# Two expert positions of a mixture-of-experts block in column tiles of 32

## The chip, the cores and the metric

The kernel runs on one core of one Trainium2 chip. The metric is the device time of one execution in microseconds, the median of several runs. The profile is one further execution, taken by the hardware profiler.

## What is computed

The reference is one decoder layer on 512 tokens of width 1024: RMSNorm, an input projection, a pooling mixer and latent attention side by side, an output projection with residual, and then a mixture of experts with residual and a final RMSNorm. The part that matters here is the mixture:

```python
logits = (ht @ w_router + b_router).astype(jnp.float32)      # 32 experts
top_vals, top_idx = lax.top_k(logits, TOP_K)                  # 4 per token
gates = jax.nn.softmax(top_vals, axis=-1)
...
gu = xblk @ w_gate_up[e] + b_gate_up[e]                       # 1024 -> 2 x 1024
gate = jnp.minimum(gu[:, :D_EXPERT], SWIGLU_LIMIT)
up = jnp.clip(gu[:, D_EXPERT:], -SWIGLU_LIMIT, SWIGLU_LIMIT)
act = gate * jax.nn.sigmoid(SWIGLU_ALPHA * gate) * (up + 1)
return act @ w_down[e] + b_down[e]                            # 1024 -> 1024
```

Each expert works on the tokens that chose it, and its rows are added to those tokens, times the gate. All of it is float32. With the reference's inputs, the two experts that the last two positions get have 31 and 22 tokens.

## The kernel before

The mixer and attention take the first fifth of the time. After the routing, the experts are ranked by their number of tokens and put on 32 **positions**. `KINDS` gives each position a kind: the big ones ("B") have 104 or 128 slots for tokens, the small ones ("S") 64. Positions 0 and 1 are fixed experts, the twelve big positions come next by size and alternate with small ones, and positions 26 to 31 are all small, with position 31 (`E - 1`) the last. If an expert has more tokens than its position has slots, a loop at the end (`tc.For_i`) takes the rest in further blocks of 128; `capc` is the number of slots by rank.

A position has eight **gate-up items** (128 rows of `w_gate_up`, 1 MB each) and four **down items** (256 rows of `w_down`, 1 MB; for position 31, `load_down_last`, a half of the output columns and 512 rows each). The SP queue loads each item into one of nine slots, in a fixed order, as soon as a slot is free. A planner (`interleave`) writes the order of all items out by hand; TensorE (PE) keeps that program order (`InOrder`). Between items `step()` advances other work by one piece: the selection and the gathering of tokens, the transposes (`turn`), and the scatter pairs (`combine`: two matmuls add one pair of positions to 128 tokens by 512 columns, then DVE adds the result to `y`, line 1157).

In a small position a matmul has the tokens as its stationary operand, 64 columns wide, and a row block of the weights as the moving one, 512 columns at a time. Its output has 64 partitions, so two matmuls lie side by side in one PSUM bank: in `gate_up` the column blocks c = 0, 1 (gate) share one bank and c = 2, 3 (up) another, on partitions `64 * (c % 2)`. `swiglu` takes the two banks as 128 partitions by 512; `turn` transposes the result and copies it to `at` (line 1044), and `down` multiplies it with `w_down`, the two column halves q side by side in a bank `db`.

When a small position's four down items are done, ACT scales the two halves of `db` into `ysh` (line 1107), DVE takes the rest into `ysl` (line 1109) and writes the scatter matrices `ss0`, `ss1` (line 1105). Two small positions share these tiles: one has columns 0 to 511 on partitions 0 to 63, the other on 64 to 127. Position 30 (`E - 2`) has no partner, since position 31 is treated alone in `down_last`; DVE therefore writes zeros to the other half of the tiles first (line 1103). These tiles have one buffer, so the writes wait until the pair before (28 and 29) has been scattered.

`down_last` runs for position 31 and column half c = 0, then 1: eight matmuls into a bank, even k on partitions 0 to 63 and odd k on 64 to 127 as partial sums (the scatter adds them), eight scatter matmuls of position 30, the copies to `ybh` and `ybl`, eight scatter matmuls of position 31, the additions to `y` (line 1139) and the final norm (`final_norm`), ending with four writes of the output.

At the end, PE's order is: the last six of the 16 gate-up items of positions 30 and 31, each with a scatter pair of positions 28 and 29 behind it; the spreading of `g_final` (`spread`, four matmuls with one row); the seventh scatter pair; the transposes of position 30; its first down item; the eighth scatter pair; two down items; the transposes of position 31; the last down item; `down_last`.

Of the kernel before, what the change touches and what calls it, by code (L numbers as in the profile page):

```python
# [24 lines left out]
P = 128  # L25
# [102 lines left out]
def block_kernel(ctx: ExitStack, tc: tile.TileContext, xT, x, pos, vecs, w_in, w_pool, w_qb, w_kvb, w_out,  # L128
# [656 lines left out]
    def bank(tag):  # L785
        return pools["pm"].tile([P, T], F32, tag=tag, bufs={"x": 4, "y": 2, "m": 2}[tag], name=tag)
# [59 lines left out]
    def big(r):  # L846
        return r == "o" or KINDS[r] == "B"

    def slots_of(r):
        return CAP if r != "o" and big(r) and KINDS[:r].count("B") >= NFULL else P  # L850

    def onx(r):

        return big(r) or r == 0 or r == E - 1

    def select(r, ovc=None):

        oh = mo.tile([P, NT, P], F16, tag="oh", bufs=2, name="oh")
        src = ovc[:, :, 0] if r == "o" else posm[:, :, r]
        for t in range(NT):  # L860
            if big(r):
                n = slots_of(r)
                V.tensor_scalar(oh[:, t, 0:n], iota_s[:, 0:n], src[:, t:t + 1], None, op0=ALU.is_equal)
            else:
                V.tensor_scalar(oh[:, t, :].rearrange("p (a b) -> p a b", a=2),  # L865
                                iota_s[:, 0:64].unsqueeze(1).to_broadcast([P, 2, 64]), src[:, t:t + 1], None,
                                op0=ALU.is_equal)
        onehot[r] = oh

# [92 lines left out]
    def biases(r, cs):  # L962
        for c in cs:
            bs = bias[:, c * T:(c + 1) * T]
            if big(r):
                PE.matmul(banks[r][c], lhsT=m4b[0:96, r:r + 1].to_broadcast([96, slots_of(r)]), rhs=bs, start=True, stop=False)
            else:
                q = 64 * (c % 2)
                PE.matmul(banks[r][c // 2][q:q + 64, :], lhsT=m4b[0:96, r:r + 1].to_broadcast([96, 64]), rhs=bs,
                          start=not fixed(r), stop=fixed(r))  # L970

    def gate_up(r, k):

        first = r == "o"
        if k == 0:
            banks[r] = [bank("x" if onx(r) else "y")[0:slots_of(r)] for _ in range(4 if big(r) else 2)]
        if big(r):

            todo = [(hf, c) for hf in range(2) for c in range(2)] if k < KD - 1 else [
                (hf, c) for c in range(2) for hf in range(2)]  # L980
            parts = presplit.pop((r, "gu", k))
            for n, (hf, c) in enumerate(todo):
                cs = slice(c * T, (c + 1) * T)
                if k == 0 and not first:
                    biases(r, [2 * hf + c])
                mm3(PE, banks[r][2 * hf + c], xg[r][0][:, k, :], xg[r][1][:, k, :], parts[hf][0][:, cs],
                    parts[hf][1][:, cs], first and k == 0, k == KD - 1)
                if n == 1:
                    yield
        else:  # L990
            w = wslots.pop((r, "gu", k))
            for c in range(4):
                q = 64 * (c % 2)
                if k == 0 and c % 2 == 0 and not fixed(r):
                    biases(r, [c, c + 1])
                PE.matmul(banks[r][c // 2][q:q + 64, :], lhsT=xg[r][:, k, :], rhs=w[:, c * T:(c + 1) * T],
                          start=(k == 0 and fixed(r)), stop=(k == KD - 1 and not fixed(r)))

                if k == KD - 1 and c % 2 == 1 and fixed(r):
                    biases(r, [c - 1, c])  # L1000

    def swiglu(gb, ub, gbias=None, ubias=None):
        n = gb.shape[0]
        g = mo.tile([P, T], F32, tag="ag", bufs=1, name="ag")[0:n]
        sg = mo.tile([P, T], F32, tag="as", bufs=1, name="as")[0:n]
        u = mo.tile([P, T], F32, tag="au", bufs=2, name="au")[0:n]
        if gbias is not None:
            V.tensor_tensor(g, gb, gbias, op=ALU.add)
            V.tensor_tensor(u, ub, ubias, op=ALU.add)
            gb, ub = g, u  # L1010
        V.tensor_scalar(g, gb, 7.0, None, op0=ALU.min)  # L1011
        S.activation(sg, g, AF.Sigmoid, scale=1.702)  # L1012
        V.tensor_scalar(u, ub, 7.0, -7.0, op0=ALU.min, op1=ALU.max)  # L1013
        V.scalar_tensor_tensor(u, u, 1.0, g, op0=ALU.add, op1=ALU.mult)  # L1014
        V.tensor_tensor(u, u, sg, op=ALU.mult)  # L1015
        return u

    def act(r):
        b = banks.pop(r)
        return [swiglu(b[c], b[2 + c]) for c in range(2)] if big(r) else [swiglu(*b)]  # L1020

    def turn(r, us_):

        if big(r):
            n = slots_of(r)
            hi, lo = (mo.tile([P, KD, P], F32R, tag=tag, bufs=1, name=tag)[:, :, 0:n] for tag in ("ath", "atl"))
            actT[r] = hi, lo
        else:
            at = mo.tile([P, 2, 4, 64], F32, tag="ath" if onx(r) else "ats", bufs=1, name="ats")
            actT[r] = at.rearrange("p a b s -> p (a b) s")  # L1030
        for c, u in enumerate(us_):
            if c:
                yield
            tp = bank("m")
            for j in range(4):
                n = slots_of(r)
                PE.transpose(tp[:, j * P:j * P + n], u[:, j * P:(j + 1) * P], ident[0:n, 0:n])
            if big(r):
                v = tp.rearrange("p (a b) -> p a b", b=P)[:, :, 0:n]
                S.copy(hi[:, 4 * c:4 * c + 4, :], v)  # L1040
                V.tensor_tensor(lo[:, 4 * c:4 * c + 4, :], v, hi[:, 4 * c:4 * c + 4, :].bitcast(F32),
                                op=ALU.subtract)
            else:
                S.copy(at, tp.rearrange("p (b a s) -> p a b s", b=4, a=2))  # L1044

# [3 lines left out]
    def down(r, j):  # L1049
# [30 lines left out]
        else:  # L1080
# [3 lines left out]
            for k in range(2 * j, 2 * j + 2):  # L1084
                for q in range(2):
                    c = q ^ par
                    PE.matmul(db[64 * q:64 * q + 64, :], lhsT=at[:, k, :], rhs=w[:, k - 2 * j, c * T:(c + 1) * T],
                              start=(k == 0), stop=(k == KD - 1))
            if not last:
# [6 lines left out]
            halfdone[0] = r if halfdone[0] is None else None  # L1096
            yh, yl = yb["s"]
            places = [(slice(64 * q, 64 * q + 64), q ^ par) for q in range(2)]
            if r == E - 2:
                for (ps_, c) in places:  # L1100
                    other = slice(64 - ps_.start, 128 - ps_.start)
                    for v in (yh[other, c], yl[other, c], scat["s"][c][other, :]):
                        V.tensor_scalar(v, iota_t[other, :], 0.0, None, op0=ALU.mult)
            for ps_, c in places:
                V.tensor_scalar(scat["s"][c][ps_, :], iota_t[ps_, :], slots[r][ps_, 5:6], None, op0=ALU.is_equal)  # L1105
            for ps_, c in places:
# [5 lines left out]
    def down_last(r, gf):  # L1112

        at = actT.pop(r)
        yh = mo.tile([P, 2, T], F32R, tag="ybh", bufs=1, name="ybh")
        yl = mo.tile([P, 2, T], F32R, tag="ybl", bufs=1, name="ybl")
        sc = mo.tile([P, T], F32R, tag="sc", bufs=1, name="sc")
        V.tensor_scalar(sc, iota_t, slots[r][:, 5:6], None, op0=ALU.is_equal)
        after = final_norm(gf)
        for c in range(2):  # L1120
            cs = slice(c * T, (c + 1) * T)
            db = bank("y")
            for k in range(KD):

                q = 64 * (k % 2)
                PE.matmul(db[q:q + 64, :], lhsT=at[:, k, :], rhs=wslots[r, "last", k, c], start=(k < 2),
                          stop=(k >= KD - 2))

            pb = [bank("x") for _ in range(NT)]
            for t in range(NT):  # L1130
                for i, v in enumerate(yb["s"]):
                    PE.matmul(pb[t], lhsT=scat["s"][c][:, t * P:(t + 1) * P], rhs=v[:, c], start=(i == 0), stop=False)
            S.activation(yh[:, c], db, AF.Copy, scale=slots[r][:, 6:7])
            V.scalar_tensor_tensor(yl[:, c], db, slots[r][:, 6:7], yh[:, c].bitcast(F32), op0=ALU.mult,
                                   op1=ALU.subtract)
            for t in range(NT):
                for i, v in enumerate((yh, yl)):
                    PE.matmul(pb[t], lhsT=sc[:, t * P:(t + 1) * P], rhs=v[:, c], start=False, stop=(i == 1))
                V.tensor_tensor(y[:, t, cs], y[:, t, cs], pb[t], op=ALU.add)
                after(t, c)  # L1140
# [129 lines left out]
    def ordering():  # L1270
# [59 lines left out]
        for n, v in ((NFIX + NFULL, P - CAP), (NFIX, 64 - P)):  # L1330
            V.tensor_scalar(capf, rank, float(n), float(v), op0=ALU.is_lt, op1=ALU.mult)
            V.tensor_tensor(capc, capc, capf, op=ALU.add)
        V.tensor_scalar(capc, capc, 64.0, None, op0=ALU.add)
        over = rp.tile([P, 1], F32, name="over")
        V.tensor_tensor(over, cn[:, E:E + 1], capc, op=ALU.subtract)
        nblk = rp.tile([P, 1], F32, name="nblk")
# [347 lines left out]
```

## Time and profile before

| | |
|---|---|
| median of 3 runs | 1263.69 us (1263.1 to 1264.01) |
| the profiled execution | 1273.83 us |
| its span, first to last instruction | 1272.1 us |
| mean granted TensorE clock | 0.978 of 2.4 GHz |
| busy: PE, DVE, ACT, POOL | 1212.4, 863.7, 540.5, 304.1 us |
| read from HBM | 428.92 MB, 341 GB/s over the span |

PE is TensorE's matmuls and PEld its weight loads, DVE is VectorE, ACT ScalarE, POOL GpSimd, and SP the engine whose queue issues the loads. PE's ends are modelled, so a busy PE is not PE at its peak. The profiled execution is some 10 us longer than the runs; durations are taken from it and sums are made against it.

### The profile page before, as it was taken

The page shows a single profiled execution, that of the slowest core. Times are in us where ns is not written, and L with a number is a line of the kernel's source. Part 1 is how long each engine was busy: PE and PEld are TensorE (multiplying, and loading weights), DVE is VectorE, ACT ScalarE, POOL GpSimd, SP SyncE. Part 2 cuts the span into 40 slices and gives each one's busy share as a digit, 9 for nine tenths or more (in the row PEclk, how much of TensorE's full clock was granted, in tenths as well). Part 3 has the DMA queues.
Part 4 walks back from the last instruction along what each step waited for, and adds up shares of the span by engine and source line. Part 5 has one row for each costly group of instructions (what it writes and reads, how often), then busy time and mean ns, then how long its engine had stood idle before and what let it go on. Part 6 is the DMA issues. An engine that isn't in the chain of part 4 may idle for free.

```text
span 1272.1 us, 16527 instructions
## 1 busy us (share of the span) xinstructions
PE 1212.4 (95%) x5597; PEld 678.3 (53%) x5597; DVE 863.7 (68%) x1555; ACT 540.5 (42%) x785; POOL 304.1 (24%) x272
## 2 busy tenths in 40 slices
PE   7979988899999998999989999999999999999994
PEld 6856773345556555555545455555545555555332
DVE  6897574656868686676768767876765876866344
ACT  6457640044435444454344524444434454444013
POOL 2355361112121121222114112231312121222001
PEclk9999998899999999999989999999989999999988
DMA  8312428999999998999998999999999999999971
GB/s 312 100 51 89 143 100 326 345 412 415 416 417 402 420 390 333 366 392 415 399 373 350 390 409 379 417 393 402 368 410 369 353 422 392 398 394 405 421 304 68
DMA packets 86850, 434.38 MB, mean 341 GB/s; under 512 B 9416, under 2 KB 9416, under 8 KB 53993
## 3 DMA queue, kind: packets, MB, share of 16 engines
q1 hardware_dynamic: 82818, 420.43, 83.6%
q0 software_dynamic: 3744, 12.45, 2.8%
q8 instruction: 45, 0.74, 0.2%
q10 hardware_dynamic: 198, 0.39, 0.1%
q14 instruction: 45, 0.36, 0.1%
HBM read 428.92 MB, written 4.33 MB: 341 GB/s over the span
## 4 chain that ended last, share of the span: by engine, by line
PE 71%; DVE 10%; DMA 1%; issue 1%; ACT 1%; POOL 0%; DVEq 0%; ACTq 0%; POOLq 0%
PE x L120 32%; PE y L120 28%; PE m L120 11%; DVE mlo L944 4%; DMA bdraw<-in_b_down_dram 1%; DVE au L1014 1%; ACT mhi L943 1%; DVE au L1015 1%; DVE oh L865 1%; DVE ag L1011 1%; DVE au L1013 0%; DVE ss L1105 0%; DVE y L1157 0%; DVE xgl L900 0%; DVE ysl L1109 0%
## 5 line engine op out<-in xcount | busy, mean ns | idle before, releaser
L943 ACT CAST mhi<-slot 128x1024 fp32r<-128x1024 f32 x288 | 300.7, 1049 | 257.1 <-PE x L120 243.1
L944 DVE TENSOR_TENSOR mlo<-slot,mhi 128x1024 fp32r<-128x1024 f32 x216 | 288.1, 1346 | 63.6 <-ACT mhi L943 63.1
L944 POOL TENSOR_TENSOR mlo<-slot,mhi 128x1024 fp32r<-128x1024 f32 x72 | 177.5, 2466 | 640.5 <-ACT mhi L943 640.4
L120 PE MATMUL y<-slot,xgs 128*64 128x512 f32 x1152 | 276.4, 602 | 0.0
L1157 DVE TENSOR_TENSOR y<-y,m 128x512 f32<-128x512 f32 x168 | 114.9, 684 | 120.9 <-PE m L120 120.5
L120 PE MATMUL x<-mhi,xgh 128*104 128x512 f32 (+1 forms) x384 | 163.1, 425 | 0.0
L120 PE MATMUL x<-mlo,xgh 128*104 128x512 f32 (+1 forms) x384 | 151.1, 394 | 0.4 <-DVE mlo L944 0.4
L120 PE MATMUL x<-mhi,xgl 128*104 128x512 f32 (+1 forms) x384 | 151.3, 394 | 0.0
L120 PE MATMUL y<-slot,ats 128*64 128x512 f32 x608 | 146.1, 617 | 0.7 <-ACT ats L1044 0.7
L120 PEld LDWEIGHTS y<-slot,xgs 128*64 128x64 f32 x1152 | 76.2, 137 | 129.8 <-issue 125.0
L1012 ACT ACTIVATE as<-ag 128x512 f32<-128x512 f32 (+1 forms) x44 | 27.8, 631 | 164.3 <-DVE ag L1011 164.3
L120 PEld LDWEIGHTS x<-mhi,xgh 128*104 128x104 f32 (+1 forms) x384 | 67.3, 175 | 31.4 <-issue 12.2
L120 PEld LDWEIGHTS y<-slot,ats 128*64 128x64 f32 x608 | 40.3, 140 | 76.0 <-issue 72.0
L120 PEld LDWEIGHTS x<-mlo,xgh 128*104 128x104 f32 (+1 forms) x384 | 67.3, 175 | 21.0 <-DVE mlo L944 1.8
L120 PEld LDWEIGHTS x<-mhi,xgl 128*104 128x104 f32 (+1 forms) x384 | 67.0, 174 | 21.3
L120 PE MATMUL x<-mhi,ath 128*104 128x512 f32 (+1 forms) x192 | 63.6, 413 | 0.0
L120 PE MATMUL x<-mlo,ath 128*104 128x512 f32 (+1 forms) x192 | 61.0, 399 | 0.0
L120 PE MATMUL x<-mhi,atl 128*104 128x512 f32 (+1 forms) x192 | 60.7, 398 | 0.0
L1107 ACT ACTIVATE ysh<-y,sl 64x512 fp32r<-64x512 f32 x36 | 24.6, 683 | 80.8 <-PE y L120 80.5
L1109 DVE SCALAR_TENSOR_TENSOR ysl<-y,sl,ysh 64x512 fp32r<-64x512 f32 x36 | 27.0, 750 | 43.3 <-ACT ysh L1107 42.8
L887 POOL DMA_INDIRECT xr<-hrow,idx x21 | 29.2, 1390 | 96.5 <-DVE idx L884 48.3
L899 ACT ACTIVATE xgh<-m,gs 128x104 fp32r<-128x104 f32 (+1 forms) x96 | 32.1, 352 | 33.5 <-PE m L120 17.0
(402 smaller groups left out, 1728.3 us busy)
## 6 DMA issues: line engine op xcount, KB each, us to landing
slot<-in_w_gate_up_dram SPq DMA_DIRECT2D x256, 1024.0 KB, 10.3
slot<-in_w_down_dram SPq DMA_DIRECT2D x128, 1024.0 KB, 9.5
wraw<-in_w_in_dram SPq DMA_DIRECT2D x16, 256.0 KB, 5.4
wraw<-in_w_out_dram SPq DMA_DIRECT2D x16, 256.0 KB, 2.6
xtraw<-in_xT_dram SPq DMA_DIRECT2D x8, 256.0 KB, 5.2
y<-in_x_dram SPq DMA_DIRECT2D x4, 512.0 KB, 7.1
hrow<-part POOLq DMA_DIRECT2D x8, 256.0 KB, 3.6
out_dram<-o SPq DMA_DIRECT2D x4, 512.0 KB, 2.7
```

Of the source, the lines that this page charges most:

```text
L120: r = f(*args, **kwargs)
L865: V.tensor_scalar(oh[:, t, :].rearrange("p (a b) -> p a b", a=2), iota_s[:, 0:64].unsqueeze(1).to_broadcast([P, 2, 64]), src[:, t:t + 1], ...
L887: G.indirect_dma_start(out=rows[r], out_offset=None, in_=hrow, in_offset=bass.IndirectOffsetOnAxis(ap=idx[0:slots_of(r), 0:1], axis=0), bo ...
L899: S.activation(hi[:, d, :], v, AF.Copy, scale=g)
L943: S.copy(hi, src)
L944: eng.tensor_tensor(lo, src, hi.bitcast(F32), op=ALU.subtract)
L1011: V.tensor_scalar(g, gb, 7.0, None, op0=ALU.min)
L1012: S.activation(sg, g, AF.Sigmoid, scale=1.702)
L1014: V.scalar_tensor_tensor(u, u, 1.0, g, op0=ALU.add, op1=ALU.mult)
L1107: S.activation(yh[ps_, c], db[ps_, :], AF.Copy, scale=slots[r][ps_, 6:7])
L1109: V.scalar_tensor_tensor(yl[ps_, c], db[ps_, :], slots[r][ps_, 6:7], yh[ps_, c].bitcast(F32), op0=ALU.mult, op1=ALU.subtract)
L1157: V.tensor_tensor(y[:, t, cs], y[:, t, cs], pb, op=ALU.add)
```

## The change

Positions 30 and 31 get 32 slots instead of 64. The one-hot selection matrix of such a position repeats its 32 slots four times over the 128 partitions (before: 64 slots twice). The four column blocks of a gate-up item go to the four quarters of one bank, each matmul with a stationary operand of 32 columns, so gate lies on partitions 0 to 63 and up on 64 to 127. `swiglu` works on 64 partitions. In position 30's second product the two column halves of an even k lie on quarters 0 and 1 and those of an odd k on quarters 2 and 3, as partial sums; position 31's has k modulo 4 on the four quarters. The scaling, the subtraction and the scatter matrix of position 30 are written in four pieces of 32 partitions instead of two of 64. The zeros are written to the whole tiles, by POOL. `capc` subtracts 32 for the last two ranks.

```diff
+    def quarter(r):
+        return r != "o" and r >= E - 2
...
+                a = 4 if quarter(r) else 2
+                V.tensor_scalar(oh[:, t, :].rearrange("p (a b) -> p a b", a=a),
+                                iota_s[:, 0:P // a].unsqueeze(1).to_broadcast([P, a, P // a]), src[:, t:t + 1], None,
...
+            elif quarter(r):
+                PE.matmul(banks[r][0][32 * c:32 * c + 32, :], lhsT=m4b[0:96, r:r + 1].to_broadcast([96, 32]), rhs=bs,
+                          start=True, stop=False)
...
+            banks[r] = [bank("x" if onx(r) else "y")[0:slots_of(r)] for _ in range(4 if big(r) else 1 if quarter(r) else 2)]
...
+        elif quarter(r):
+            w = wslots.pop((r, "gu", k))
+            if k == 0:
+                biases(r, range(4))
+            for c in range(4):
+                PE.matmul(banks[r][0][32 * c:32 * c + 32, :], lhsT=xg[r][:, k, 0:32], rhs=w[:, c * T:(c + 1) * T],
+                          start=False, stop=(k == KD - 1))
...
+        if quarter(r):
+            return [swiglu(b[0][0:64, :], b[0][64:P, :])]
...
+            actT[r] = at.rearrange("p a b s -> p (a b) s")[:, :, 0:32 if quarter(r) else 64]
...
+                n = 64 if quarter(r) else slots_of(r)
...
+            elif quarter(r):
+                S.copy(at[:, :, :, 0:32], tp.rearrange("p (b a s) -> p a b s", b=4, a=4)[:, 0:2])
...
+                    if quarter(r):
+                        o = 32 * (2 * (k % 2) + q)
+                        PE.matmul(db[o:o + 32, :], lhsT=at[:, k, :], rhs=w[:, k - 2 * j, q * T:(q + 1) * T],
+                                  start=(k < 2), stop=(k >= KD - 2))
+                        continue
...
-            if r == E - 2:
-                for (ps_, c) in places:
-                    other = slice(64 - ps_.start, 128 - ps_.start)
-                    for v in (yh[other, c], yl[other, c], scat["s"][c][other, :]):
-                        V.tensor_scalar(v, iota_t[other, :], 0.0, None, op0=ALU.mult)
+            if quarter(r):
+                places = [(slice(32 * (2 * a + c), 32 * (2 * a + c) + 32), c) for a in range(2) for c in range(2)]
+                for c in range(2):
+                    for v in (scat["s"][c], yh[:, c], yl[:, c]):
+                        G.tensor_scalar(v, iota_t, 0.0, None, op0=ALU.mult)
...
-                q = 64 * (k % 2)
-                PE.matmul(db[q:q + 64, :], lhsT=at[:, k, :], rhs=wslots[r, "last", k, c], start=(k < 2),
-                          stop=(k >= KD - 2))
+                q = 32 * (k % 4)
+                PE.matmul(db[q:q + 32, :], lhsT=at[:, k, :], rhs=wslots[r, "last", k, c], start=(k < 4),
+                          stop=(k >= KD - 4))
...
-        V.tensor_scalar(capc, capc, 64.0, None, op0=ALU.add)
+        V.tensor_scalar(capf, rank, float(E - 2), -32.0, op0=ALU.is_ge, op1=ALU.mult)
+        V.scalar_tensor_tensor(capc, capc, 64.0, capf, op0=ALU.add, op1=ALU.add)
```

## Rows read from the trace of the kernel before

**Rows 1.** The page: DMA's busy share in 40 slices, and the chain by engine.
```profile
DMA  8312428999999998999998999999999999999971
...
PE 71%; DVE 10%; DMA 1%; issue 1%; ACT 1%; POOL 0%; DVEq 0%; ACTq 0%; POOLq 0%
```

**Rows 2.** Windows: stretch, busy us per engine (instructions), PEclk, DMA share, GB/s.
```profile
1200.30:1225.70 25.40, 25.40 (x107) 8.00 (x105) 9.22 (x14) 0.63 (x1) 0.00 (x0) 1.00 1.02 410
...
1225.70:1229.80 4.10, 3.42 (x12) 1.36 (x11) 3.46 (x6) 2.39 (x4) 0.00 (x0) 0.87 1.05 387
1229.80:1235.60 5.80, 5.80 (x14) 1.69 (x16) 1.53 (x4) 0.00 (x0) 0.00 (x0) 0.50 0.52 194
1235.60:1244.50 8.90, 8.90 (x44) 2.83 (x40) 3.27 (x7) 1.95 (x3) 0.00 (x0) 1.00 0.01 2
```

**Rows 3.** The chain that ended last, from 1223 us on: start, us, what.
```profile
1223.22 0.67 PE m L120 x2
1223.88 1.87 PE x L120 x8
1225.75 2.58 PE m L120 x6
...
1233.48 1.15 PE m L120 x2
...
1244.58 3.90 PE x L120 x16
1248.47 3.58 PE y L120 x16
```

**Rows 4.** Timeline of the SP queue: load issues, start and duration.
```profile
1207.18 16.45 SPq L808 DMA_DIRECT2D slot<-in_w_down_dram  x8
...
1215.67 2.90 SPq L808 DMA_DIRECT2D slot<-in_w_down_dram  x2
```

**Rows 5.** DMA issues at 1207.18 and at 1215.67: count, KB, us to landing.
```profile
slot<-in_w_down_dram SPq DMA_DIRECT2D x1, 1024.0 KB, 9.1
...
slot<-in_w_down_dram SPq DMA_DIRECT2D x1, 1024.0 KB, 11.0
```

**Rows 6.** Window of one us at the end of the loads.
```profile
1234.00:1235.00 1.00, 1.00 (x4) 0.30 (x4) 0.73 (x2) 0.00 (x0) 0.00 (x0) 0.50 0.01 2
```

**Rows 7.** Timeline of the matmuls of `spread`, 128 columns wide.
```profile
1225.68 1.98 PE L120 MATMUL m<-gf,ones 1*128 1x512 f32 x4
...
1226.22 0.18 PEld L120 LDWEIGHTS m<-gf,ones 1*128 1x128 f32 x1 [0.24 <-issue]
1226.65 0.18 PEld L120 LDWEIGHTS m<-gf,ones 1*128 1x128 f32 x1 [0.24 <-issue]
```

**Rows 8.** Timeline of one gate-up item of position 31, 64 columns wide.
```profile
1200.96 1.94 PE L120 MATMUL x<-slot,xgs 128*64 128x512 f32 x8
...
1201.44 0.14 PEld L120 LDWEIGHTS x<-slot,xgs 128*64 128x64 f32 x2 [0.29 <-issue]
1201.87 0.14 PEld L120 LDWEIGHTS x<-slot,xgs 128*64 128x64 f32 x2 [0.28 <-issue]
```

**Rows 9.** Timeline of the router's products, 32 columns wide, 128 moving columns.
```profile
183.70 0.74 PE L120 MATMUL lga<-xk,wr 128*32 128x128 f32 x10
```

**Rows 10.** Timeline of DVE's zeros and what ended the wait before them.
```profile
1234.24 0.87 DVE L1103 TENSOR_SCALAR ysh<-iota_t 64x512 fp32r<-64x512 f32 x2 [4.24 <-PE m L120]
```

**Rows 11.** Groups by line and shape: busy us, mean ns, idle before.
```profile
L647 POOL TENSOR_SCALAR part<-y,r2s 128x512 f32<-128x512 f32 x8 | 13.4, 1681 | 10.2 <-DVE r2s L100 9.9 <-PE tp L120 0.2
L1184 POOL TENSOR_TENSOR o<-y,gf 128x512 f32<-128x512 f32 x4 | 5.0, 1285 | 74.8 <-issue 74.8
L1109 DVE SCALAR_TENSOR_TENSOR ysl<-y,sl,ysh 64x512 fp32r<-64x512 f32 x36 | 27.0, 750 | 43.3 <-ACT ysh L1107 42.8
L936 DVE TENSOR_SCALAR sl<-sl 128x1 f32<-128x1 f32 x24 | 4.9, 203 | 0.1
L1107 ACT ACTIVATE ysh<-y,sl 64x512 fp32r<-64x512 f32 x36 | 24.6, 683 | 80.8 <-PE y L120 80.5
```

More of the change, by code (lines that the diff above doesn't have):

```diff
@@ L864, in select @@
             else:
-                V.tensor_scalar(oh[:, t, :].rearrange("p (a b) -> p a b", a=2),
-                                iota_s[:, 0:64].unsqueeze(1).to_broadcast([P, 2, 64]), src[:, t:t + 1], None,
+                a = 4 if quarter(r) else 2
+                V.tensor_scalar(oh[:, t, :].rearrange("p (a b) -> p a b", a=a),
+                                iota_s[:, 0:P // a].unsqueeze(1).to_broadcast([P, a, P // a]), src[:, t:t + 1], None,
                                 op0=ALU.is_equal)
@@ L975, in gate_up @@
         if k == 0:
-            banks[r] = [bank("x" if onx(r) else "y")[0:slots_of(r)] for _ in range(4 if big(r) else 2)]
+            banks[r] = [bank("x" if onx(r) else "y")[0:slots_of(r)] for _ in range(4 if big(r) else 1 if quarter(r) else 2)]
         if big(r):
@@ L1029, in turn @@
             at = mo.tile([P, 2, 4, 64], F32, tag="ath" if onx(r) else "ats", bufs=1, name="ats")
-            actT[r] = at.rearrange("p a b s -> p (a b) s")
+            actT[r] = at.rearrange("p a b s -> p (a b) s")[:, :, 0:32 if quarter(r) else 64]
         for c, u in enumerate(us_):
@@ L1035, in turn @@
             for j in range(4):
-                n = slots_of(r)
+                n = 64 if quarter(r) else slots_of(r)
                 PE.transpose(tp[:, j * P:j * P + n], u[:, j * P:(j + 1) * P], ident[0:n, 0:n])
```

## The prediction

> **What bounds the kernel now.** I read the page first: the chain that ended last is 71% TensorE work, and in the line by slices the DMA engines are nine tenths busy or more almost to the end [rows 1]. Two things run level, so the stage that the change touches has to be read by itself. That stage is the last 24 loads of 1 MB: 16 gate-up items of positions 30 and 31 (eight each), four down items of 30, four of 31. The windows of that stretch [rows 2] show both at their limit: from 1200.3 to 1225.7 PE is busy for 25.40 of 25.40 us and the DMA share is 1.02 at 410 GB/s. Then the loads end, and PE alone carries the time: the chain of waits [rows 3] is PE from 1223.9 to 1252, with no wait for a load in it. So PE sets the end, and the loads run a little ahead of it. How far ahead decides this case.
>
> The lead: the first down load of position 30 is issued at 1207.18 and lands 9.1 us later, at 1216.3; the first of position 31 is issued at 1215.67 and lands 11.0 later, at 1226.7 [rows 4, 5]. One MB (1.049 million bytes) at 410 GB/s takes 2.56 us, so the 16th gate-up load, the one before 1216.3, lands at 1213.7; PE begins its item at 1223.9 [rows 3], 10.2 us later. With the 387 GB/s that the window from 1225.7 shows, 2.7 us each, the last three loads land at 1229.4, 1232.1 and 1234.8; the traffic is at 2 GB/s in 1234 to 1235 [rows 6], which agrees. The loads cannot come sooner: their share is already 1.0.
>
> **The matmuls: what they cost, and how many run at once.** A float32 matmul is two instructions here. Across the whole array one takes 0.43 us: the four of `spread` fill 1.98 us and their weight loads come 0.43 apart [rows 7]. With 64 columns, weight loads come in twos every 0.43 us, and eight instructions end within 1.94 us [rows 8], so two tiles work side by side. A gate-up item (eight instructions) is thus 4 x 0.43 = 1.72 us. Whether four tiles of 32 columns work side by side, no row shows. Below: tiles of 32 columns do run at least in twos, since ten `lga` matmuls of 128 columns end within 0.74 us [rows 9], where one after another they would take 10 x 0.107 (0.43 / 4) = 1.07. So the item costs between 1.72 (two at once, no gain) and 0.86 (four). I take 0.86: in [rows 8] a second tile costs the first one nothing, and the four write different partitions of one bank as the two did.
>
> The Trainium skill ("TensorE: Matmul & The Clock Gate", Part 3, measured speedups) gives 2.38 times for three column tiles of 32 by 512; if four kept that rate per tile, the item would be 3.43 / 3.17 = 1.08 us by that page, and the sum below would not move, since the loads bind first. No row here shows three or four tiles.
>
> **PE's own saving.** 16 gate-up items x 0.86 = 13.7; each position's second products are 32 instructions, 16 x 0.43 = 6.9 us, halved to 3.4, twice: 6.9. Together 20.6 us at most.
>
> **What the loads take back.** Without waits the 16th item would begin at 1223.9 - 15 x 0.86 = 1211.0. Its load lands at 1213.7, so PE catches up with the loads around the 13th item and follows them from there. The order on PE is fixed, so I walk it. Item 16 ends at 1214.8 (0.86 and 0.2 to drain). Then come the six matmuls and transposes of 1225.75 and the wait for the copy, 4.1 us before (1225.7 to 1229.8): to 1218.9. Down item 0 of position 30 and the last scatter pair of the pair before (1233.48; 0.66 at full clock [rows 3]) end at 1220.5. Items 1 to 3 follow their loads at 2.56 us each; the fourth lands at 1224.0 and is done at 1225.0. Position 31's first half needs 1226.7 and 1229.4: done at 1229.4 + 0.86 + 0.17 = 1230.4. Behind it in program order stand 16 scatter matmuls, 3.9 us (1244.58 in [rows 3]): 1234.3. The second half takes 1.72, its last load having come at 1234.8: done by 1236.0. Before, that point is 1252.06 (1248.47 + 3.58). What follows it is the same work, 20.0 us to the end of the span. Gain at full clock: 16.0 us. By the load alone the floor is 1235.8.
>
> **The half clock.** In 1225.7 to 1229.8 PE ran the four one-row matmuls of `spread`, a scatter pair, transposes, and waited 0.7; the granted clock averages 0.87 there, 0.50 (1.2 GHz) in 1229.8 to 1235.6, and 1.00 after [rows 2]. In the new kernel the same stretch lies at 1214.8 to 1218.9, and a fall of equal length ends by 1226, in front of waits for loads, where it is free. But PE will then work only about 0.86 of each 2.6 us, where before it was busy throughout as the clock came back. Nothing below 0; at worst the 1.2 GHz lasts from 1229.4 to the end of the second half: 0.86 + 3.9 + 1.72, and 2 more behind it, 8 us. I take 1.5.
>
> **The zeroing and the quarters.** Six DVE writes of zeros on 64 partitions go (0.43 each, the first two waiting for the last scatter pair [rows 10]); six POOL writes over 128 partitions come. POOL's tensor-scalar of that size takes 1.68, its tensor-tensor 1.29 [rows 11]. One needs only the seventh scatter pair, five must wait for the eighth (1220.5): 5 x 1.68 = 8.4, to 1228.9, with nothing else in POOL's queue. The quarter copies take four ACT writes of 0.68 and four DVE subtractions of 0.75 instead of two each [rows 11]; from 1225.0 the ACT ones run to 1227.7. The third subtraction, which the first scatter of position 31's half 0 waits for, ends two times 0.75 after the zeros: 1230.4, exactly when PE is ready. With 1.29 it is hidden (1228.4); if the eighth pair is late at half clock it costs up to 2. I take 0.5. The Trainium skill ("TensorEngine Tiling (Array Packing)", PSUM Bottleneck) warns that tiling speeds up TensorE and not the evacuation; by that rule this chain would be next after the loads, and the rows put it level with them.
>
> **At nothing.** `select` issues as many writes of as many columns. The gate/up arithmetic keeps its 512 columns on half the partitions; the copy after the transposes shrinks, at most 0.3 us, in front of waits for loads. The capacity sum in `ordering` gains one DVE operation on one column, 0.20 by a like row [rows 11], while PE has position 0 and 1's products to run; uncovered it is 0.2. No queue is passed by a moved DMA.
>
> **Sum.** 16.0 - 1.5 - 0.5 = 14.0 us. The profiled execution took 1273.83 us (span 1272.1): 1259.8. The runs' median, 1263.69, is 10.1 below it; I carry the microseconds over: **1249.7**.
>
> **Rivals.**
> *Half clock to the end, or partial overlap.* PE stays at 1.2 GHz through position 31's closing products: 16.0 - 8 - 2 = 6 us gained, 1257.7. For it: the clock fell at this place before [rows 2]. Against: the last 6 us are dense. Three tiles' worth of overlap instead of four saves two thirds, 13.7, inside the forecast.
> *Two at a time, as now.* Then PE saves nothing, and the loads are never caught: about 1264, no measurable change (within 0.2% is 2.5 us either way). For it: no row shows more than two. Against: the tiles' weights and outputs are as separate as those of the two.
> *Evacuation binds.* If a POOL write took 3 us, the zeros would end at 1235.5 and half 0's scatter would start 6 us late: 1256. Its rows say 1.3 to 1.7.
> *Slower: tiles of 32 columns wait for each other.* If each instruction took its 0.43 alone, an item would be 3.43, the 48 pairs would cost 20.6 more, and the time 1284. It decides from less than two at once; [rows 9] speaks against.
> *Slower: the slots don't suffice.* A 33rd token sends that expert through the overflow loop: twelve loads at 2.56, 31 us or more, 1280 and above. Counted by the reference's routing, the last two positions have 31 and 22 tokens.
> *More.* Without the profiler the loads may run further ahead; PE's own saving less the losses is 18.6: 1245.1.
>
> **Chances.** Forecast, 1247 to 1252: 0.55. Half clock, late evacuation or poor overlap, 1252 to 1259: 0.24. Two at a time: 0.10. More than 16.5 gained: 0.05. Slower: 0.06. So faster 0.84, same 0.10, slower 0.06. The range from 1245 (18.6 gained) to 1257.7 leaves out the two slow rivals, the unchanged time and a little of the second case: 0.8.
>
> **What the profile after would show.** Eight instructions of a gate-up item within about 1.1 us, weight loads in fours or more; PE waiting for loads from about 1206 and its last down item right behind the last landing near 1234.8; six POOL writes of zeros of 1.3 to 1.7 us ending before 1230; the span near 1258. Wrong: weight loads still in twos every 0.43 us; a clock of 0.50 past 1232; twelve more loads behind position 31's, for the overflow loop; or a PE wait in front of the `ss` scatter that names DVE or ACT.

## The result, and the profile after

The changed kernel takes 1253.67 us (median of 4, 1252.86 to 1257.45), the kernel before in the same series 1263.85 (median of 4): a ratio of 0.992, 95% interval 0.9905 to 0.9935, so 10.2 us less (8.2 to 12.0). The forecast was 1249.7, 14.0 less: right in sign, 4 us too much. The first profile of the changed kernel is an execution of 1257.45 us (span 1255.7), its second (below) one of 1252.68 (span 1251.0).

The measure used throughout is the **closing stretch**: from the first gate-up matmul of position 31 to the end of the span. In the profile that stands ahead of the prediction it is 1272.1 - 1187.8 = 84.3 us, in the first profile after 1255.7 - 1182.3 = 73.4.

Timeline of PE in the changed kernel, with what ended the wait in brackets (the counterpart of [rows 8]):

```profile
1196.63 1.06 PE L120 MATMUL x<-slot,xgs 128*32 128x512 f32 x8
...
1199.84 1.06 PE L120 MATMUL y<-slot,xgs 128*32 128x512 f32 x8 [1.48 <-DMA slot<-in_w_gate_up_dram]
...
1202.15 1.06 PE L120 MATMUL y<-slot,xgs 128*32 128x512 f32 x8 [0.58 <-DMA slot<-in_w_gate_up_dram]
...
1222.69 1.06 PE L120 MATMUL y<-slot,ats 128*32 128x512 f32 x8 [0.76 <-DMA slot<-in_w_down_dram]
1225.31 1.91 PE L120 MATMUL y<-slot,ats 128*32 128x512 f32 x8 [1.55 <-DMA slot<-in_w_down_dram]
...
1228.43 0.77 PE L120 MATMUL x<-ysl,ss 128*128 128x512 f32 x1 [0.48 <-DVE ysl L1135]
...
1233.80 1.92 PE L120 MATMUL y<-slot,ats 128*32 128x512 f32 x16
```

Eight instructions end within 1.06 us where they took 1.94, and from 1199.8 on PE waits in front of most items for their load. The weight loads show how many run at once, in fours per 0.43 us where [rows 8] have twos:

```profile
1218.63 0.16 PEld L120 LDWEIGHTS y<-slot,ats 128*32 128x32 f32 x8 [0.65 <-issue]
1219.08 0.13 PEld L120 LDWEIGHTS y<-slot,ats 128*32 128x32 f32 x4 [0.30 <-issue]
1219.51 0.13 PEld L120 LDWEIGHTS y<-slot,ats 128*32 128x32 f32 x4 [0.30 <-issue]
```

The windows of the same stretch answer to [rows 2] (busy us per engine, then PEclk, DMA share, GB/s):

```profile
1195.00:1200.00 5.00, 3.52 (x28) 1.04 (x24) 1.37 (x2) 0.00 (x0) 0.00 (x0) 1.00 1.02 419
...
1210.00:1215.00 5.00, 5.00 (x18) 1.67 (x10) 3.17 (x5) 1.80 (x3) 0.37 (x1) 0.67 1.02 408
...
1220.00:1225.00 5.00, 3.00 (x28) 0.67 (x20) 0.69 (x1) 3.09 (x5) 5.00 (x4) 1.00 1.05 387
1225.00:1230.00 5.00, 4.21 (x13) 1.78 (x14) 4.73 (x7) 0.69 (x1) 0.73 (x1) 0.54 0.67 249
1230.00:1235.00 5.00, 5.00 (x25) 3.17 (x27) 2.48 (x6) 1.75 (x5) 1.65 (x2) 0.78 0.00 0
```

The DMA share stays at 1.0 to 1225 while PE is busy for only 3 to 3.5 of 5 us in two of these windows: the loads now lead. There are two falls of the granted clock, one in 1210 to 1220 in front of waits, one in 1225 to 1235 (0.54, 0.78), where PE's work sets the end. The chain of waits, counterpart of [rows 3], ends through the zeros:

```profile
1221.37 1.45 POOL ysl L1129
1222.82 1.46 POOL ss L1129
...
1224.31 0.82 DVE ss L1131
...
1226.02 0.74 DVE ysl L1135
...
1228.43 5.45 PE x L120 x15
1233.87 1.85 PE y L120 x16
```

### The profile page after: what moved, and what is told of

Same layout as the page of the kernel before. It is cut to its first block, busy times and chain, and to the rows that moved or that the text cites. A ratio compares the mean times of both kernels' runs of the same rounds, so it can differ in the third digit from the quotient of the medians.

```text
span 1255.7 us, 16536 instructions
## 1 busy us (share of the span) xinstructions
PE 1192.4 (95%) x5597; PEld 671.4 (53%) x5597; DVE 864.3 (69%) x1554; ACT 541.2 (43%) x787; POOL 313.1 (25%) x278
## 3 DMA queue, kind: packets, MB, share of 16 engines
HBM read 428.92 MB, written 4.33 MB: 345 GB/s over the span
## 5 line engine op out<-in xcount | busy, mean ns | idle before, releaser
L120 PE MATMUL y<-slot,xgs 128*64 128x512 f32 (+1 forms) x1152 | 269.3, 602 | 2.8 <-DMA slot<-in_w_gate_up_dram 2.8
L120 PEld LDWEIGHTS y<-slot,xgs 128*64 128x64 f32 (+1 forms) x1152 | 73.5, 135 | 128.6 <-issue 119.9
L120 PE MATMUL y<-slot,ats 128*64 128x512 f32 (+1 forms) x608 | 138.6, 620 | 2.8 <-DMA slot<-in_w_down_dram 2.3
L1027 ACT ACTIVATE as<-ag 128x512 f32<-128x512 f32 (+2 forms) x44 | 27.8, 631 | 158.1 <-DVE ag L1026 158.1
L120 PEld LDWEIGHTS y<-slot,ats 128*64 128x64 f32 (+1 forms) x608 | 37.2, 136 | 72.9 <-issue 66.9
L1133 ACT ACTIVATE ysh<-y,sl 64x512 fp32r<-64x512 f32 (+1 forms) x38 | 25.9, 682 | 80.7 <-PE y L120 80.4
L1135 DVE SCALAR_TENSOR_TENSOR ysl<-y,sl,ysh 64x512 fp32r<-64x512 f32 (+1 forms) x38 | 28.5, 749 | 38.1 <-ACT ysh L1133 37.6
```

The source lines that it names most:

```text
L120: r = f(*args, **kwargs)
L1133: S.activation(yh[ps_, c], db[ps_, :], AF.Copy, scale=slots[r][ps_, 6:7])
L1135: V.scalar_tensor_tensor(yl[ps_, c], db[ps_, :], slots[r][ps_, 6:7], yh[ps_, c].bitcast(F32), op0=ALU.mult, op1=ALU.subtract)
```

## The experiments

The last column is the closing stretch in the profile of that run. Expectations that name 84.6 and 73.6 us count the stretch in the two first profiles from the bias matmuls, some 0.2 us earlier.

| run | median us (runs) | ratio to before, 95% | closing stretch |
|---|---|---|---|
| before again | 1264.21 (1) | | 81.4 |
| changed kernel again | 1253.27 (6) | 0.9927, 0.9908 to 0.9946 | 70.5 |
| gate-up items alone | 1255.77 (5) | 0.9929, 0.9908 to 0.9949 | 73.3 |
| second products alone | 1263.4 (10) | 0.9995, 0.9982 to 1.0007 | 80.5 |
| the same, short evacuation | 1259.34 (5) | 0.9963, 0.9950 to 0.9976 | 77.4 |
| before, four loads less | 1264.26 (10) | 0.9998, 0.9988 to 1.0008 | 81.1 |
| changed, four loads less | 1251.81 (4) | 0.9909, 0.9892 to 0.9925 | 69.3 |
| the same, short evacuation | 1248.23 (4) | 0.9878, 0.9864 to 0.9893 | 65.7 |
| changed, zeros on DVE | 1253.18 (6) | 0.9916, 0.9891 to 0.9942 | 69.5 |
| changed, waits filled | 1254.68 (5) | 0.9915, 0.9895 to 0.9934 | 73.4 |
| changed, both of these | 1254.68 (5) | 0.9916, 0.9896 to 0.9935 | 71.6 |
| changed, short evacuation | 1252.95 (6) | 0.9913, 0.9899 to 0.9928 | 71.7 |

**The kernel before, unaltered, a second profile.**

> The kernel before, unchanged, profiled once more: its first profile lost 5.9 us to the changed kernel's already in the routing stage, where ACT's second cast of b_down began at 213.6 us against 205.3. If that was one late load: the cast begins near 205 now, the closing stretch is 84.6 within 0.5, and the span is some 6 us shorter. If it belongs to the kernel before: 213 again.

Its closing stretch is 1262.4 - 1181.0 = 81.4 us, 2.9 less than in the first profile. The windows of this second profile:

```profile
1225.00:1230.00 5.00, 5.00 (x24) 1.75 (x25) 3.10 (x7) 0.28 (x1) 0.00 (x0) 1.00 0.15 55
1230.00:1235.00 5.00, 5.00 (x25) 1.53 (x21) 1.50 (x2) 1.67 (x3) 0.00 (x0) 1.00 0.02 3
```

The clock is 1.00 behind `spread` where [rows 2] have 0.50 for 5.8 us. The three other profiles with gate-up items of two tiles (the second products alone, the same with the short evacuation, before with four loads less) show 1.00 from 1205 to 1230 as well. The later series list the mean granted clock of 52 further executions of the kernel before: 51 have 0.982 to 0.987 and one 0.979, where the first profile has 0.978. So that fall belongs to a rare execution, not to the kernel's usual course. The rest of what the first profile was too long lies before the stretch (1187.8 against 1181.0, 6.8 us): a late load of `b_down` held up the routing, with 17.1 us of waiting for it in the chain that ended last; in the second profile it is not in that chain. ACT's timeline in the first profile of before:

```profile
213.57 0.62 ACT L1258 CAST bd<-bdraw 96x512 fp32r<-96x512 f32 x1 [11.84 <-DMA bdraw<-in_b_down_dram]
```

and in the second:

```profile
206.56 0.62 ACT L1258 CAST bd<-bdraw 96x512 fp32r<-96x512 f32 x1 [4.41 <-DMA bdraw<-in_b_down_dram]
```

**The changed kernel, unaltered, a second profile.**

> The changed kernel, unaltered, for a second profile of it. Theory: the runs' gain of 10.2 us lies in the closing stretch, and the first profile of the changed kernel (stretch from position 31's first gate-up item to the end 73.4 us, 1257.45 us, where the runs' median was 1253.67) caught a second fall of the clock that not every execution has. The kernel before has a stretch of 81.5, so this one should show 70.5 to 72.5 without a second half-clock stretch, or 73 to 74 with one, and its time should differ by the same 2 to 3 us. Rival, that the stretch is 73 to 74 in every execution, with or without that fall, so that 2 us of the gain come from before it: then the time up to position 31's first item is 2 us below that of the kernel before (about 1180.9 us in its second profile) in this profile too.

PE's timeline in it:

```profile
1180.47 1.03 PE L120 MATMUL x<-slot,xgs 128*32 128x512 f32 x8
...
1221.72 1.07 PE L120 MATMUL y<-slot,ats 128*32 128x512 f32 x8 [1.55 <-DMA slot<-in_w_down_dram]
1224.03 0.76 PE L120 MATMUL x<-ysl,ss 128*128 128x512 f32 x1 [0.81 <-DVE ysl L1135]
1229.03 1.92 PE L120 MATMUL y<-slot,ats 128*32 128x512 f32 x16
```

The stretch is 70.5. It begins at 1180.5, 0.5 us from the 1181.0 of before: the gain, 81.4 - 70.5 = 10.9 us, lies in the closing stretch, and the rival falls. So the number of the theory came, but not its condition. A second fall of the clock is there too, only shorter: the window from 1225 shows 0.80 where the first profile had 0.54.

```profile
1225.00:1230.00 5.00, 5.00 (x26) 3.34 (x28) 2.71 (x5) 1.53 (x5) 1.43 (x2) 0.80 0.09 33
```

The last load of position 31's first half also came earlier: its matmuls start 41.2 us into the stretch, against 43.0 (1225.31 - 1182.31) in the first profile. The chain that ended last is another one as well; the zeros are not in it:

```profile
1211.07 1.94 PE y L120 x8
...
1214.15 3.16 PE y L120 x16
...
1218.82 0.68 ACT ysh L1133
...
1223.13 0.76 DVE ysl L1135
...
1224.03 5.07 PE x L120 x15
```

It runs through position 30's down items, which the first fall of the clock slows, then ACT's four copies, DVE's subtractions and the scatter. From the first down item to the first copy it takes 7.75 us (1211.07 to 1218.82); the second products alone, with the same items at full clock, take 5.3 (1222.04 to 1227.34). So executions of the same program spread over 3 us here, by the loads and by the clock.

**The gate-up items alone.** The second products stay 64 columns wide; each token stands twice and its gate is halved. Position 30's zeros and its evacuation are those of before.

```diff
-    actT[r] = at.rearrange(...)[:, :, 0:32 if quarter(r) else 64]
+    actT[r] = at.rearrange(...)
-    S.copy(at[:, :, :, 0:32], ...)
+    for o in (0, 32):
+        S.copy(at[:, :, :, o:o + 32], ...)
+    V.tensor_scalar(sl[:, 6:7], sl[:, 6:7], 0.5, None, op0=ALU.mult)
```

> Only the gate-up products in four tiles of 32; the second products, the two pieces of position 30 and DVE's zeros as before the change (each slot stands twice and its gate is halved, so the output is the same). TensorE saves 13.7 us of the 20.6. If the loads bind: nothing lost in position 30's down items; only position 31's last products are 2.6 us longer at full clock, and what the clock and the zeros cost can come back, so 72.6 to 76.2. If TensorE's saving counted by its size: two thirds of 11.0, 77.3.

Some 8.4 us of the gain is there (1264.2 - 1255.8), and the stretch of 73.3 lies in the range of the loads theory (72.6 to 76.2), not at the 77.3 of the other.

**The second products alone.** The gate-up items, `swiglu` and the transposes are those of before.

```diff
-    elif quarter(r):
-        ... (gate-up in four tiles, biases, one bank)
```

> Only the second products in four tiles (and POOL's zeros in four pieces); gate-up in two tiles of 64 as before. TensorE saves 6.9 us and never catches the loads in the gate-up items, so by the loads theory all 6.9 show: stretch from position 31's first item to the end 84.6 - 6.9 = 77.7 us, less if the clock does not fall. If the saving counted by its share of the whole: a third of 11.0, 81.0.

No gain that can be measured, and a stretch of 80.5 where 77.7 was expected; from the 81.4 of the second profile of before, the saving of 6.9 would give 74.5, so 6.0 of the 6.9 are missing. The wait that took it is in the timeline of POOL, DVE and PE:

```profile
1229.52 1.49 POOL L1117 TENSOR_SCALAR ysl<-iota_t 128x512 fp32r<-128x512 f32 x1
1229.59 1.70 DVE L1119 TENSOR_SCALAR ss<-iota_t,sl 32x512 fp32r<-32x512 f32 x2 [5.09 <-POOL ss L1117]
...
1231.30 3.05 DVE L1123 SCALAR_TENSOR_TENSOR ysl<-y,sl,ysh 32x512 fp32r<-32x512 f32 x4
1233.71 0.73 PE L120 MATMUL x<-ysl,ss 128*128 128x512 f32 x1 [3.74 <-DVE ysl L1123]
```

DVE's scatter quarters wait 5.09 us for POOL's zeros, the subtractions come behind them, and PE idles 3.74 us, and 0.57 one matmul earlier. The clock fell in that wait (0.87 and 0.78 in the two windows from 1230), and the scatter behind it took some 1.6 us longer. Together that is about the missing 6.0. Here the rival "evacuation binds" is the case.

**The same with a short evacuation.** DVE writes the zeros, and the column halves are evacuated one after the other, so that the first scatter needs two subtractions and not three of four.

```diff
-    G.tensor_scalar(v, iota_t, 0.0, None, op0=ALU.mult)
+    V.tensor_scalar(v, iota_t, 0.0, None, op0=ALU.mult)
-    places = [... for a in range(2) for c in range(2)]
+    places = [... for c in range(2) for a in range(2)]
-    (four ACT copies, then four DVE subtractions)
+    (two copies, two subtractions for c = 0; then the same for c = 1)
```

> The second products alone in quarters, as in the run of that part before, but the zeros are written by DVE and the scaling, the subtraction and the scatter run column half by column half, so that the first scatter needs two copies and two subtractions and not four. Theory: in that part's run PE waited 4.3 us for the third subtraction behind POOL's zeros, and the clock fell in the wait. DVE is free at 1224.5 in its times, writes five zeros of 0.42 and four scatter quarters of 0.48 (beside no POOL work), ACT has the first half at 1228.7, so the subtractions end near 1230.2 where they ended at 1233.7: the stretch from position 31's first gate-up item falls from 80.5 to 75.5 to 77, the time to 1258 to 1260. Rival, that half-size second products save nothing here because something else (the loads, or the closing work) sets the end: stretch 80 or more, time 1262 to 1264.

```profile
1226.94 0.98 DVE L1119 TENSOR_SCALAR ss<-iota_t,sl 32x512 fp32r<-32x512 f32 x2
...
1229.64 1.50 DVE L1124 SCALAR_TENSOR_TENSOR ysl<-y,sl,ysh 32x512 fp32r<-32x512 f32 x2 [1.73 <-ACT ysh L1122]
...
1231.20 0.50 PE L120 MATMUL x<-ysl,ss 128*128 128x512 f32 x1 [0.88 <-DVE ysl L1124]
```

PE's wait is 0.88 (timeline above), and the second products alone now bring 4.5 us (1263.79 - 1259.34). So the wait came from the zeros and the evacuation; which of the two edits did how much is not separated here. The run also had no fall of the clock, so part of the 4.1 us between the two runs is that. The short order has a price: DVE now does the second half's subtractions in front of position 31's, and PE waits another 0.24 and 1.12 us before that scatter.

**Four loads less.** The odd gate-up row blocks of position 30 use the block before; the matmuls stay.

```diff
+    if what == "gu" and r == E - 2 and k % 2:
+        wslots[r, "gu", k] = wslots[r, "gu", k - 1]
```

In the kernel before:

> The kernel before with the same four loads left out. TensorE bound it, with the loads 10 us ahead: 84.6 us within 0.5. If loads bound the kernel before too: several us less.

In the changed one:

> The changed kernel with four gate-up loads of position 30 left out (odd row blocks use the block before, so position 30's result is another). All later loads land some 10 us sooner. If the loads bind the change: TensorE's whole saving of 20.6 shows, less the clock and the zeros, stretch 64 to 67 us. If they don't: 73.6.

Before, four loads (10 us of transfer) less change nothing: PE set the end. In the changed kernel the waits for loads are gone, yet it is only 1.9 us faster (1253.67 - 1251.81), which the overlapping intervals do not show to be a difference. The stretch is 69.3 where 64 to 67 was expected, because the next limit is right behind. Its timeline:

```profile
1217.25 1.49 POOL L1129 TENSOR_SCALAR ysl<-iota_t 128x512 fp32r<-128x512 f32 x1
...
1218.54 0.74 DVE L1135 SCALAR_TENSOR_TENSOR ysl<-y,sl,ysh 32x512 fp32r<-32x512 f32 x1 [6.12 <-ACT ysh L1133]
1219.29 0.98 DVE L1131 TENSOR_SCALAR ss<-iota_t,sl 32x512 fp32r<-32x512 f32 x2
1220.29 2.29 DVE L1135 SCALAR_TENSOR_TENSOR ysl<-y,sl,ysh 32x512 fp32r<-32x512 f32 x3
...
1221.94 0.77 PE L120 MATMUL x<-ysl,ss 128*128 128x512 f32 x1 [3.65 <-DVE ysl L1135]
```

**The same with the short evacuation** (the edit above on top):

> The changed kernel with four gate-up loads of position 30 left out (its odd row blocks use the block before) as in the earlier run, with the zeros on DVE and the evacuation column half by column half. Theory: with the loads out of the way the zeros and quarters of position 30 bound that run (PE waited 4.2 us for them, its loads had landed); with DVE's zeros the first subtractions end near 1218.5 in its times where they ended at 1221.9. Stretch 65 to 66.5 where it was 69.3, time 1247.5 to 1249.5. Rival, that PE itself or the clock sets the end once the loads are out of the way: stretch 68.5 to 69.5, time 1251 to 1252.

1248.23, another 3.6 us, with the wait at 0.89 (timeline):

```profile
1217.43 1.50 DVE L1136 SCALAR_TENSOR_TENSOR ysl<-y,sl,ysh 32x512 fp32r<-32x512 f32 x2 [2.34 <-ACT ysh L1134]
...
1218.98 0.50 PE L120 MATMUL x<-ysl,ss 128*128 128x512 f32 x1 [0.89 <-DVE ysl L1136]
```

The clock, 0.50 from 1220 to 1225 in the run before, did not fall here, so part of the 3.6 is that.

So in the changed kernel the loads and the evacuation of position 30 are nearly level. In both its profiles the chain that ended last goes through the evacuation: PE, done with the item of the last load, still waits 0.48 and 0.81 us for it. Taking away one alone brings nothing that stands clear of the scatter (the loads 1.9 us, the evacuation 0.7, in the last experiment below); both together bring 5.4 (1253.67 - 1248.23). With the short evacuation and in one series, the four loads are worth 4.7 (1252.95 - 1248.23). What PE alone would allow no run shows: the last one still waits 0.89, 0.24 and 1.12 us for the evacuation.

**The zeros on DVE, the waits filled, both.** The first edit is the `G` to `V` line above. The second adds matmuls into a bank that nobody reads, behind `spread` and in front of position 30's down items and position 31's first half:

```diff
+    def warm(n):
+        for _ in range(n):
+            PE.matmul(fill[0], lhsT=onesb[0:96, :], rhs=bias[:, 0:T], start=True, stop=True)
```

> The six writes of zeros go from POOL back to DVE, over whole tiles. Measure: the stretch from position 31's first gate-up item to the end of the span, 84.6 us before and 73.6 after the change. Theory A (three things stand between the stretch and the loads alone: 2.8 us of half clock, 0.85 of waiting for DVE's third subtraction behind POOL's zeros, 1.3 of loads that land later): the 0.85 goes, 72.7. Rival L (the loads alone set the end): 73.6, no difference. Rival Z (the zeros set the end): 2 us or more, under 71.6.

> The changed kernel with 22 bf16 matmuls of 96 x 128 by 512 (0.21 us each at full clock) that write a spare bank nobody reads, put into TensorE's waits from the spreading of g_final to position 31's first half. Theory A: the granted clock stays 1.00 from 1210 us to the last product, 2.8 us come back, and since the eighth scatter pair is sooner the zeros end sooner too: up to 3.6 us, stretch 70.0 to 71.5. Rival L (loads alone): 73.6. Rival Z (POOL's zeros bind in any case): at most 1 us, 72.6.

> Both: zeros by DVE, and the matmuls that fill the waits. Theory A: 3.6 us less than the change, stretch 70.0, within 0.5 of the fill alone. Rival Z: much less than the fill alone. Rival L: 73.6.

With the zeros on DVE (0.42 us each) the profile has no second fall of the clock and a stretch of 69.5, but PE still waits 0.60 us, now because DVE's four subtractions follow all four of ACT's copies (timelines of PE):

```profile
1223.80 0.50 PE L120 MATMUL x<-ysl,ss 128*128 128x512 f32 x1 [0.60 <-DVE ysl L1135]
...
1227.46 1.92 PE L120 MATMUL y<-slot,ats 128*32 128x512 f32 x16
```

The runs' median is 0.5 us below the changed kernel's, inside the scatter. Filling the waits keeps the clock at 1.00 from 1220 on (windows of that run):

```profile
1225.00:1230.00 5.00, 4.91 (x31) 1.32 (x27) 3.61 (x5) 3.17 (x5) 2.45 (x2) 1.00 0.63 228
```

but the time is not better (1254.68 with either place of the zeros), and the first fall, around `spread`, comes all the same (1212.3 to 1219.1). The filling has a price of its own: in the chain that ended last of that run the added matmuls stand with 4.3 us. So these two runs do not tell what the falls cost.

**The whole change with the short evacuation.**

> The changed kernel whole, all loads, zeros on DVE and the evacuation column half by column half. Theory: with all loads the last landing sets position 31's last product, and DVE's zeros alone left a PE wait of 0.6 us at the first scatter; that wait goes and nothing else. Stretch 68.8 to 69.5, time 1252 to 1253. Rival, that the order of the halves matters beyond the wait that the trace shows (the zeros run: 1253.18): below 1251.5.

1252.95: no measurable gain over the changed kernel, as forecast for the time. Its stretch, 71.7, is above the forecast: the wait for DVE is gone, but the loads came as late as in the first profile (43.2 us into the stretch), and the clock fell without any wait for zeros (timeline, then a window):

```profile
1223.87 1.93 PE L120 MATMUL y<-slot,ats 128*32 128x512 f32 x8 [1.56 <-DMA slot<-in_w_down_dram]
```

```profile
1225.00:1230.00 5.00, 5.00 (x19) 3.47 (x16) 2.12 (x4) 0.91 (x2) 0.13 (x1) 0.77 0.36 133
```

That also ends the reading that the wait for the zeros makes the second fall: here PE waited for loads alone, 1.56 us, and it fell. No version was found that beats the changed kernel with all its loads.

## Why the prediction was right, and its size off

**Four at once, as forecast.** An item takes 1.06 us to its last end and its weight loads come in fours per 0.43, so the steady rate is the 0.86 that the prediction took. "Two at a time" and the slower rival of waiting tiles are out. By the estimate that the prediction worked out from the Trainium skill ("TensorE: Matmul & The Clock Gate", Part 3, 2.38 times for three tiles) an item would be 1.08 us at the steady rate; this case's 0.86 shows full overlap of four instead.

**The loads take it back, as forecast.** PE's 20.6 us were to shrink to 16.0 because PE catches up with the loads. It does (waits from 1199.8 on), and with the loads thinned out the kernel gains clearly more only once the evacuation is shortened too (1251.81, 1248.23). The walk through PE's order was good: it put the matmuls for the last load of position 31's first half 41.7 us into the stretch (1229.4 - 1187.75), and the two profiles have 41.2 and 43.0. What follows the second half takes 20.0 us in both kernels, as it said. The second half itself does not follow its load, as the prediction had it (last landing 47.0 us into the stretch): it starts 51.5 and 48.6 us into it, behind the scatter and with no wait for a load.

**The step that failed is the half clock**, and with it the size of the 16.0. It read [rows 2], 0.50 in 1229.8 to 1235.6, as a part of the kernel, and the sum set "Before, that point is 1252.06" against a new kernel in which "a fall of equal length ends by 1226 ... where it is free". The second profile of before shows a stretch of 81.4 instead of 84.3 with no such fall. So 2.9 of the 16.0 us were an accident of that execution, which the usual run did not contain and no change could win: 16.0 should have been 13.1, and 13.1 - 1.5 - 0.5 = 11.1 is inside the measured 8.2 to 12.0. The forecast of the new stretch itself, 84.3 - 14.0 = 70.3, is met by the second profile (70.5). The warning was in the table: the execution was 10.1 us over the median, and the prediction carried the microseconds over without asking where the 10 lay. Some 2.9 of them lay in the stretch that it costed, 6.8 before it.

**The clock after the change** was put at 1.5 us, bounds 0 to 8, a value chosen between them and not worked out. The falls behind position 31's first half cost between nothing (zeros on DVE: none) and some 3 us (first profile: an item at 1.91 instead of 1.06, and eight scatter matmuls 0.43 apart instead of 0.23). In the second, the 16 scatter matmuls and their waits took 6.3 us (1222.7 to 1229.0) where 3.9 was reckoned, 0.8 of it the wait for DVE. That leaves 1.6, so 1.5 fits that execution, by luck as much as by reckoning. The first fall, which was to be free in front of waits for loads, is not quite: in the second profile it slows the down items of position 30, and PE's 0.81 us of waiting for the evacuation stands behind them. Two of the prediction's signs of being wrong did come, a clock of 0.50 past 1232 (in its times) and a wait in front of the `ss` scatter that names DVE; both cost about what it had set aside for them (1.5 and 0.5 us), save the clock in the first profile. What makes the clock fall there is open: filled waits kept it up, but of two runs with the same wait for the last load, zeros on DVE (1.55 us) and short evacuation (1.56), the first had no fall and the second had one.

**Zeros and quarters** were put at 0.5, bounds 0 to 2: PE waits 0.48 and 0.81. The POOL write is 1.49 us, between the 1.29 and 1.68 of [rows 11]; the five took 7.3 us where 8.4 was reckoned. Only in the first profile do the zeros end the wait; in the second it is the four copies and the subtractions. "Evacuation binds" was close by: it is what undoes the second products alone, and the next limit once loads are taken away. The Trainium skill has the rule that tiling speeds up TensorE and not the evacuation ("TensorEngine Tiling (Array Packing)", PSUM Bottleneck). The two runs with the short evacuation agree with it: they are 4.1 and 3.6 us faster than those without, the zeros and the clock included.

**The other rivals.** Half clock to the end (1257.7): not in the median, though the first profile, 1257.45, comes near. The overflow loop: the profile's page after shows 428.92 MB read, as before, so no further loads. "More" (1245.1) lies outside the interval.

## What to carry to other kernels

Before summing against a profiled execution that is longer than the runs, find where it is longer: take the stretch that the change touches from a second profile, or leave out what a clock fall put into it. A matmul that becomes twice as fast pays only up to the next thing that was nearly level with it; here that was the loads, and level with them the zeroing and evacuation of one position. Half a change can be worth nothing (the second products alone) because a helper that came with it, here POOL's zeros and the evacuation behind them, takes the gain, so test the halves with and without the helper.

## What the runs showed of the hardware

- The same write of zeros, 128 by 512 float32, takes 1.49 us on POOL and 0.42 on DVE. Two DVE comparisons on 32 partitions took 1.70 us beside a POOL write (1229.59 above; the same in both profiles of the changed kernel) and 0.98 without one (1226.94).
- Evacuating quarters saves nothing per write: a subtraction takes 0.75 us on 32 partitions as on 64 [rows 11], so four quarters cost twice two halves.
- The granted clock fell to 1.2 GHz behind `spread` in one of the five profiles with two-tile gate-up items (the first of before). In all nine profiles with four-tile gate-up items it fell, inside `spread` or within 3 us behind it. Waits for loads stood in front of it or, in the runs with four loads less, none of them. The cause is open.
